# A decoder layer in three-pass float32: around three norms, low halves of weights are held back until the first low half of the operand is set down, and the next three are queued behind it

## The chip, the cores and the metric

One core of a Trainium2 chip. The metric is the device time of one execution of the whole program, in microseconds, from the program's start to its end; three executions were timed.

## The reference

One layer of a decoder, 256 tokens by 2048 channels, all in float32:

```
x  <- LN0(a*x + 0.5*(silu(x @ A1) * (x @ U1)) @ O1)       feed-forward, 5504 wide
z  =  x @ W_in                                            convolution, recurrence and gate parts
m  =  sigmoid(gc)*(yA @ Wa) + sigmoid(gh)*(yB @ Wb)       yA: gated convolution, yB: gated recurrence
x  <- LN1(a*x + m @ W_out)
x  <- LN2(a*x + 0.5*(silu(x @ A2) * (x @ U2)) @ O2)
x  <- LN3(a*x + sigmoid(x @ W_pg) * (p @ W_pp))
```

LN is a layer norm over the 2048 channels with a scale and a shift. All weights are read once from memory, 430 MB in all.

## The kernel before

**Three matmuls for one.** Every product is made of operands that are split in a high and a low half: the high half is the value rounded to the matmul's format (a cast on ScalarE), the low half is the rest (a subtraction on VectorE). A product is the sum of three matmuls into one bank: high by high, high by low, low by high. For the weights the high half is `wh` (`weight_cast`, L1141) and the low half `wl` (`weight_split`, L1153); a piece of both is 256 rows by 512 columns, and holds for 12 matmuls, six for each of the two row tiles of 128 tokens. For the operand, which is normalized and turned before, the halves are `xh` (L302) and `xl` (L303), both made in `halves`; one pair covers four blocks of 128 channels, 12 matmuls. Feed-forward operands are named `gh` and `gl`.

**Units.** `run_unit` goes through a unit, one block of 512 output columns: for each block of channels the row tile 0, then row tile 1, three matmuls for each block of 128 channels (`passes`, L1210 and L1214). When row tile 1 has used a piece of weights, its buffers come free, and `feed` loads, casts and splits the next pieces as far as there is room: 4 raw buffers, 6 and a few more for the halves. A raw buffer is free for the next load as soon as its split is done.

**A norm.** The last unit before a norm adds its result to `x0` (row tile 0) and `x1` (row tile 1), and takes statistics by blocks of 512 columns. `layer_norm` turns these to a mean and a factor `r`, normalizes four times 512 columns in place (L496), and puts off for each of the four quarters the making of an operand: four transposes on TensorE (L289), scale and shift on ScalarE out of the bank (L490, `y` or `yT`), the cast to `xh`, the subtraction to `xl`. The first quarter of row tile 0 is what the next unit's first matmuls need. Three norms have this form: the first behind the first feed-forward part, the second behind the mixer's output product, the third behind the second feed-forward part. At the third, small units (`ple_w_proj`, `pp`, L998) lie between the norm and the first unit that needs its operand. The closing norm has no operand and is another function.

**What sets the order.** The program is written in one stream, and a scheduler orders each engine's queue by a model of the times. `issue_after(i)` tells it to put an instruction behind `i`. The table `gate` holds such wishes: `gate["lo"]` has an instruction and a count, and each split that finds the count above zero is put behind that instruction (`gated`). In the kernel before, the first two splits behind a norm's second normalizing step of row tile 0 are held behind that step. On its engine each instruction then waits in order for what it needs. SP issues the loads, in order too.

Of the kernel before, what the change touches and what calls it, by code (L numbers as in the profile page):

```python
# [10 lines left out]
F32 = mybir.dt.float32  # L11
# [3 lines left out]
ALU = mybir.AluOpType  # L15
# [14 lines left out]
LATE = (4, 12)  # L30
# [8 lines left out]
class Stat:  # L39
# [3 lines left out]
    def __init__(self):  # L43
        self.parts = {}
# [7 lines left out]
class Unit:  # L52


    def __init__(self, stat, w, row, nk, col, width, epi, split=SPLIT):
        self.stat, self.w, self.row, self.nk = stat, w, row, nk
        self.col, self.width, self.epi = col, width, epi
        self.blocks = []
        k = 0
        for n in split:  # L60
            end = min(nk, k + n)
            if k < end:
                self.blocks.append([list(range(i, min(end, i + KG))) for i in range(k, end, KG)])
            k = end
# [78 lines left out]
def hybrid_layer(ctx: ExitStack, tc: tile.TileContext, x, p, ln_g, ln_b, ffn1_w_in, ffn1_w_out, mix_w_in,  # L143
                 conv_w, hg_lower_bound, hg_norm_w, branch_w_conv, branch_w_hgrn, mix_w_out,
                 ffn2_w_in, ffn2_w_out, ple_w_gate, ple_w_proj, x_t, p_t, small_t, out):
    nc = tc.nc

    def pool(name, bufs=1, **kw):
        return ctx.enter_context(tc.tile_pool(name=name, bufs=bufs, **kw))


    low = pool("low", side="left")
    wp = pool("wp", side="left")
    op = pool("op", side="left")
# [50 lines left out]
        used_at[n] = max(used_at.values()) + 1  # L205


    state = {"tick": 0}
    later = []
    unsettled = set()  # L210
    gate = {}
    background = deque()

    def defer(delay, fn):
        insort(later, (state["tick"] + delay, fn), key=lambda e: e[0])
# [70 lines left out]
    def transposed(src, nb):  # L286
        tp = ptile("t", "tp")
        for i in range(nb):
            state["turned"] = nc.tensor.transpose(tp[:, i * P : (i + 1) * P], src[:, i * P : (i + 1) * P], ident).ins  # L289
        return tp  # L290

    def halves(stat, t, g, src, nb, tag, into=None):

        if into:
            h, l = into
        else:
            where, bufs = {"s": (region["pool"], 7), "m": (region["pool"], 4)}.get(tag, (op, 8))
            h = where.tile([P, 4, P], F32R, tag=tag + "h", name=tag + "h", bufs=bufs)
            l = where.tile([P, 4, P], F32R, tag=tag + "l", name=tag + "l", bufs=bufs)
        hf = h[:, :nb, :].rearrange("p a b -> p (a b)")  # L300
        lf = l[:, :nb, :].rearrange("p a b -> p (a b)")
        state["half"] = nc.scalar.copy(hf, src).ins  # L302
        nc.vector.tensor_tensor(out=lf, in0=src, in1=hf.bitcast(F32), op=ALU.subtract)  # L303
        stat.parts[t, g] = (h, l)

    def to_stat(stat, t, g, src, nb, tag):
# [10 lines left out]
    def plain_tile(t, c):  # L317

        if c % 2 == 0:
            plain[t, c // 2] = high(("11", "12", "21", "22")[2 * t + c // 2], "yT")  # L320
        return plain[t, c // 2][:, c % 2, :]
# [128 lines left out]
    def moments(t, scale):  # L450

        mv = st.tile([P, 2], F32, tag="mv", name="mv", bufs=2)
        nc.vector.bn_aggr(mv, stats.pop(t))
        return mv[:, 0:1], rsqrt_of(mv[:, 1:2], 1, 1.0, LN_EPS / scale ** 2)
# [23 lines left out]
    def layer_norm(t, i, scale, stat):  # L478

        mean, r = moments(t, scale)  # L480

        def operand(c, xc):
            y = plain_tile(t, c) if stat is x2 else st.tile([P, CC], F32, tag="silu", name="y", bufs=2)
            tp = transposed(xc, 4)
            if t == 0 and c < 2:
                gate["pe"] = state["turned"], 1
            with tc.issue_after(state["half"]) if c else nullcontext():
                for a in range(4):
                    k = i * 16 + 4 * c + a
                    nc.scalar.activation(y[:, a * P : (a + 1) * P], tp[:, a * P : (a + 1) * P], AF.Identity,  # L490
                                         bias=gbT[:, 48 + k : 49 + k], scale=gbT[:, k : k + 1])
            halves(stat, t, c, y, 4, "x")

        for c in range(4):
            xc = xt[t][:, c * CC : (c + 1) * CC]
            norm = nc.vector.tensor_scalar(out=xc, in0=xc, scalar1=mean, scalar2=r, op0=ALU.subtract, op1=ALU.mult)  # L496
            defer((4 if t else 5) + c, lambda c=c, xc=xc: operand(c, xc))
            if c == 1 and t == 0:
                gate["lo"] = norm.ins, 2
        if t == NT - 1:  # L500
            for c in range(4):
                unsettled.add(c)
                early = stat is x2
                defer(2 + 3 * c if early else 40 + 20 * c, lambda c=c, early=early: affine_rows(i, c, early, stat))
# [496 lines left out]
    for c in range(4):  # L1001
        def epi_s(t, acc, c=c):
# [13 lines left out]
            if c == 3:  # L1016
# [3 lines left out]
                          split=LATE if c == 3 else LONG if c == 0 else SPLIT))  # L1020
# [36 lines left out]
    cur = {"cast": 0, "split": 0}  # L1057
# [26 lines left out]
    def may_load(ring):  # L1084
        if not loads[ring]:
            return False
        if ring == "raw":
            return taken["raw"] < NRAW
        key, kind = loads[ring][0][:2]
        if ring == "12" and not key[0].shorted:  # L1090
            return False
        return kind == region["kind"] and held["on"] and (held[ring] < HIGH[ring] or key in half)
# [30 lines left out]
    def addable():  # L1123
        if not adds:
            return False
        i = adds[0]
        el = plan[i]
        if i > cur["split"] + 1 or cur["split"] <= el["behind"] or any(key not in raws for key in el["add"]):
            return False
        return el.get("short") != "h2" or held["12"] < HIGH["12"]  # L1130
# [35 lines left out]
    def feed():  # L1166
        while True:
            ring = min((r for r in loads if may_load(r)), key=lambda r: first_use[loads[r][0][0]], default=None)
            if ring:
                weight_dma(ring)  # L1170
            elif addable():
                weight_add()
            elif castable():
                weight_cast()
            elif cur["split"] < cur["cast"]:
                weight_split()
            else:
                return
# [22 lines left out]
    def consumed(i):  # L1201
        pairs.pop(i)
        room[plan[i]["where"]] += 1
        feed()
# [11 lines left out]
    def run_unit(u, gi):  # L1216
        accs = {}
        for bi, blk in enumerate(u.blocks):
            for t in range(NT):
                if bi == 0:  # L1220
                    accs[t] = ptile("a", "acc")
                acc = accs[t][:, : u.width]
                for ii, ks in enumerate(blk):
                    tick()
                    for a, k in enumerate(ks):
                        passes(acc, u.stat, t, k, gi + ii, a, k == 0, k == u.nk - 1)
                    if t == NT - 1:
                        consumed(gi + ii)
                if bi == len(u.blocks) - 1:
                    u.epi(t, acc)  # L1230
            gi += len(blk)
        return gi
# [31 lines left out]
    gi = 0  # L1264
    for u in units:
        if isinstance(u, Unit):
            gi = run_unit(u, gi)
        elif isinstance(u, Quad):
            gi = run_quad(u, gi)
# [50 lines left out]
```

## Time and profile before

| | |
|---|---|
| median of 3 runs | 2201.24 us |
| lowest, highest | 2200.41, 2201.27 us |
| the profiled execution | 2200.81 us |
| its span, first to last instruction | 2199.1 us |
| busy: TensorE, its weight loads, VectorE, ScalarE | 99%, 82%, 83%, 54% |
| loads | 430 MB, 198 GB/s over the span |

The span is the time from the first to the last instruction; some 1.7 us lie around it. The busy time of TensorE is made of matmuls that overlap, so a wait is read better from the starts of two matmuls that follow each other than from the share.

### The profile page before, as it was taken

Reading aid. Unit: us, or ns where it says so; the run is one execution under the profiler, and the core shown is the slowest. Engines: PE = TensorE matmul, PEld = TensorE weight load, DVE = VectorE, ACT = ScalarE, POOL = GpSimd, SP = SyncE. Lnnn points to the kernel's source line nnn. Section 1 sums busy time; section 2 is a strip of 40 time slices with the busy share of each in tenths; the row PEclk is TensorE's granted clock in tenths of the full one; section 3 lists DMA queues with packets and bytes.
Section 4 is the critical chain, followed back from the end, with each engine's and each line's share of the span. In section 5 each row is a group of like instructions: output and inputs, shape, how many; then the busy total and the mean of one; then the engine's idle time right before and its main releaser. Section 6 shows DMA issues by size and latency. Waiting matters only on the chain.

```text
span 2199.1 us, 27091 instructions
## 1 busy us (share of the span) xinstructions
PE 2175.5 (99%) x9996; PEld 1811.4 (82%) x9996; DVE 1827.5 (83%) x2066; ACT 1182.8 (54%) x1412; POOL 20.0 (1%) x48
## 2 busy tenths in 40 slices
PE   9999999999999999999999999999999999999997
PEld 7988888888887888888888888798888888888886
DVE  6899999999886678657898888779999989998667
ACT  5555555555555534534565554645555555555463
POOL 1000000000000000000000000000000000000000
PEclk9999999999999999999999999999999999999999
DMA  8866666566663665554665676566666666665564
GB/s 263 265 193 200 210 204 194 186 201 211 208 194 116 197 216 178 185 181 153 220 203 177 202 244 210 171 210 201 192 200 189 203 211 201 201 210 176 192 221 144
DMA packets 228245, 436.29 MB, mean 198 GB/s; under 512 B 14608, under 2 KB 23312, under 8 KB 228112
## 3 DMA queue, kind: packets, MB, share of 16 engines
q1 hardware_dynamic: 226832, 430.37, 61.7%
q0 software_dynamic: 1280, 4.20, 0.5%
q8 instruction: 78, 1.28, 0.2%
q14 instruction: 55, 0.45, 0.1%
HBM read 430.31 MB, written 4.19 MB: 198 GB/s over the span
## 4 chain that ended last, share of the span: by engine, by line
PE 95%; DVE 2%; DMA 1%; ACT 1%; issue 1%; SPq 0%; DVEq 0%; ACTq 0%
PE bank L1214 61%; PE bank L1210 31%; PE bank L289 2%; PE bank L694 1%; DVE wl L1153 1%; DMA raw<-in_ffn_w_in_dram 1%; ACT wh L1141 1%; DMA raw<-in_ffn_w_out_dram 0%; DVE x L510 0%; DVE x L511 0%; PE bank L664 0%; ACT yT L490 0%; DVE x L496 0%; DVE raw L1119 0%; DVE bn L430 0%
## 5 line engine op out<-in xcount | busy, mean ns | idle before, releaser
L1141 ACT CAST wh<-raw 128x1024 fp32r<-128x1024 f32 (+2 forms) x975 | 975.9, 1030 | 763.0 <-PE bank L1214 331.3
L1153 DVE TENSOR_TENSOR wl<-raw,wh 128x1024 fp32r<-128x1024 f32 (+2 forms) x975 | 1140.9, 1197 | 237.1 <-ACT wh L1141 224.4
L1214 PE MATMUL bank<-wh,xl 128*128 128x512 f32 (+1 forms) x1624 | 625.6, 386 | 2.8 <-DVE xl L303 1.9
L1214 PE MATMUL bank<-wl,xh 128*128 128x512 f32 (+1 forms) x1624 | 625.9, 386 | 0.4 <-DVE wl L1153 0.4
L1210 PE MATMUL bank<-wh,xh 128*128 128x512 f32 (+1 forms) x1624 | 616.0, 387 | 0.4 <-ACT xh L302 0.4
L1214 PEld LDWEIGHTS bank<-wh,xl 128*128 128x128 f32 x1624 | 304.9, 188 | 63.3 <-DVE xl L303 4.0
L1210 PEld LDWEIGHTS bank<-wh,xh 128*128 128x128 f32 x1624 | 304.9, 188 | 58.9 <-ACT xh L302 1.5
L1214 PEld LDWEIGHTS bank<-wl,xh 128*128 128x128 f32 x1624 | 305.0, 188 | 58.6 <-DVE wl L1153 1.4
L1214 PE MATMUL bank<-wl,gh 128*128 128x512 f32 x896 | 348.5, 391 | 2.3 <-DVE wl L1153 2.3
L1214 PE MATMUL bank<-wh,gl 128*128 128x512 f32 x896 | 347.9, 390 | 0.0
L1210 PE MATMUL bank<-wh,gh 128*128 128x512 f32 x896 | 345.7, 392 | 0.0
L1119 DVE TENSOR_TENSOR raw<-raw,raw 128x1024 f32<-128x1024 f32 x216 | 254.7, 1180 | 12.4 <-DMA raw<-in_ffn_w_in_dram 6.7
L1214 PEld LDWEIGHTS bank<-wl,gh 128*128 128x128 f32 x896 | 168.3, 188 | 39.0 <-DVE wl L1153 4.8
L1210 PEld LDWEIGHTS bank<-wh,gh 128*128 128x128 f32 x896 | 168.1, 188 | 35.0 <-ACT wh L1141 0.4
L1214 PEld LDWEIGHTS bank<-wh,gl 128*128 128x128 f32 x896 | 168.2, 188 | 34.9
L1214 PE MATMUL bank<-wl,sh 128*128 128x512 f32 x464 | 181.6, 391 | 0.0
L1214 PE MATMUL bank<-wh,sl 128*128 128x512 f32 x464 | 180.5, 389 | 0.0
L1210 PE MATMUL bank<-wh,sh 128*128 128x512 f32 x464 | 177.1, 389 | 0.0
L1210 PEld LDWEIGHTS bank<-wh,sh 128*128 128x128 f32 x464 | 87.1, 188 | 18.3
L1214 PEld LDWEIGHTS bank<-wh,sl 128*128 128x128 f32 x464 | 87.1, 188 | 17.8
L1214 PEld LDWEIGHTS bank<-wl,sh 128*128 128x128 f32 x464 | 87.1, 188 | 17.8
L302 ACT CAST gh<-bank 128x512 fp32r<-128x512 f32 (+1 forms) x52 | 30.1, 578 | 75.9 <-PE bank L289 75.4
(184 smaller groups left out, 1121.5 us busy)
## 6 DMA issues: line engine op xcount, KB each, us to landing
raw<-in_ffn_w_in_dram SPq DMA_DIRECT2D x287, 512.0 KB, 4.4
raw<-in_mix_w_in_dram SPq DMA_DIRECT2D x176, 512.0 KB, 4.6
raw<-in_ffn_w_out_dram SPq DMA_DIRECT2D x168, 512.0 KB, 4.8
raw<-in_ffn_w_in_dram SPq DMA_DIRECT2D x66, 256.0 KB, 2.9
raw<-in_mix_w_out_dram SPq DMA_DIRECT2D x32, 512.0 KB, 4.7
raw<-in_ple_w_gate_dram SPq DMA_DIRECT2D x32, 512.0 KB, 4.9
raw<-in_ffn_w_in_dram SPq DMA_DIRECT2D x32, 384.0 KB, 4.0
raw<-in_branch_w_conv_dram SPq DMA_DIRECT2D x16, 512.0 KB, 5.1
```

The source lines that it names most:

```text
L289: state["turned"] = nc.tensor.transpose(tp[:, i * P : (i + 1) * P], src[:, i * P : (i + 1) * P], ident).ins
L302: state["half"] = nc.scalar.copy(hf, src).ins
L694: nc.tensor.matmul(gp[:, (h * 2 + t) * 64 : (h * 2 + t + 1) * 64], kd[:, h, t * P : (t + 1) * P], qd[:, h, t, :], start=True, stop=True)
L1119: nc.vector.tensor_tensor(out=out, in0=a, in1=b, op=ALU.add)
L1141: nc.scalar.copy(h[:, ks, :w], raw[:, ks, :w])
L1153: state["split"] = nc.vector.tensor_tensor(out=l[:, ks, :w], in0=raw[:, ks, :w], in1=h[:, ks, :w].bitcast(F32), op=ALU.subtract).ins
L1210: nc.tensor.matmul(acc, sh, wh[:, a, :n], start=first, stop=False)
L1214: nc.tensor.matmul(acc, x_part, w_part[:, a, :n], start=False, stop=last and i == 1)
```

## The change

Four edits. `run_unit` marks the last units before a norm (`last`, by their split of the channels, `LATE` or `(12,)`); when row tile 0 of such a unit begins its last block, it sets a number of splits that may still be written: to the end of this unit and two pieces on. `feed` writes no split once that number is used up, and so frees no raw buffer for further loads there. `lead` takes the place of `operand` as what is put off: it makes the operand, and for the first quarter of row tile 0 it then lifts the limit, sets `gate["lo"]` to the low half just written with a count of three, and calls `feed`. `halves` keeps its subtraction in `state["low"]` for that.

```diff
 class Unit: __init__
+        self.last = split in (LATE, (12,))
...
-    state = {"tick": 0}
+    MANY = 1 << 30
+    state = {"tick": 0, "splits": MANY}
...
 def halves
-        nc.vector.tensor_tensor(out=lf, in0=src, in1=hf.bitcast(F32), op=ALU.subtract)
+        state["low"] = nc.vector.tensor_tensor(out=lf, in0=src, in1=hf.bitcast(F32), op=ALU.subtract).ins
...
 def layer_norm
+        def lead(c, xc):
+            operand(c, xc)
+            if t == 0 and c == 0:
+                state["splits"] = MANY
+                gate["lo"] = state["low"], 3
+                feed()
...
-            defer((4 if t else 5) + c, lambda c=c, xc=xc: operand(c, xc))
+            defer((4 if t else 5) + c, lambda c=c, xc=xc: lead(c, xc))
...
 def feed
-            elif cur["split"] < cur["cast"]:
+            elif cur["split"] < cur["cast"] and state["splits"] > 0:
+                state["splits"] -= 1
                 weight_split()
...
 def run_unit
+                if u.last and t == 0 and bi == len(u.blocks) - 1:
+                    state["splits"] = gi + len(blk) + 2 - cur["split"]
```

Instructions are neither added nor taken away. The order differs only around the three norms, and between them it is the same. The lines of the changed kernel stand 3 (`halves`) to 11 (`passes`) further down.

VectorE at the first norm, from behind the normalizing of row tile 0 to the second low half; `wl` is a split of weights, `xl` a low half of the operand, `x1` the addition to row tile 1. Before:

```order
L1153 TENSOR_TENSOR wl_5645<-raw_5518,wh_5644 128x1024
L1153 TENSOR_TENSOR wl_5663<-raw_5530,wh_5662 128x1024
L1153 TENSOR_TENSOR wl_5675<-raw_5548,wh_5674 128x1024
L808 MEMSET uT_6836 128x4x2
L303 TENSOR_TENSOR xl_5690<-y_5680,xh_5689 128x512
L600 TENSOR_TENSOR x1_97<-x1_97,bank6_87 128x512
L430 BN_STATS bn_5370<-x1_97 128x6
L453 BN_AGGR mv_5726<-bn_5370 128x2
L1153 TENSOR_TENSOR wl_5719<-raw_5574,wh_5718 128x1024
L438 TENSOR_SCALAR w_5728<-mv_5726 128x1
L440 TENSOR_SCALAR m_5729<-mv_5726 128x1
L303 TENSOR_TENSOR xl_5709<-y_5699,xh_5708 128x512
```

And now:

```order
L818 MEMSET uT_6836 128x4x2
L306 TENSOR_TENSOR xl_5678<-y_5668,xh_5677 128x512
L1163 TENSOR_TENSOR wl_5645<-raw_5518,wh_5644 128x1024
L1163 TENSOR_TENSOR wl_5660<-raw_5530,wh_5659 128x1024
L1163 TENSOR_TENSOR wl_5685<-raw_5548,wh_5684 128x1024
L610 TENSOR_TENSOR x1_97<-x1_97,bank6_87 128x512
L1163 TENSOR_TENSOR wl_5719<-raw_5574,wh_5718 128x1024
L306 TENSOR_TENSOR xl_5709<-y_5699,xh_5708 128x512
L433 BN_STATS bn_5370<-x1_97 128x6
L306 TENSOR_TENSOR xl_5765<-y_5755,xh_5764 128x512
```

The first `xl` has moved ahead of three splits; the statistics, the aggregate and two small steps of row tile 1 have moved behind the second `xl`. TensorE's order is the same here.

VectorE at the second norm, the same piece. Before:

```order
L1153 TENSOR_TENSOR wl_11130<-raw_11013,wh_11129 128x1024
L1153 TENSOR_TENSOR wl_11213<-raw_11025,wh_11212 128x1024
L1153 TENSOR_TENSOR wl_11216<-raw_11055,wh_11215 128x1024
L1153 TENSOR_TENSOR wl_11222<-raw_11067,wh_11221 128x1024
L303 TENSOR_TENSOR xl_11163<-yT_11153,xh_11162 128x512
L980 SCALAR_TENSOR_TENSOR x1_10356<-x1_10356,bank3_84 128x512
L1153 TENSOR_TENSOR wl_11228<-raw_11133,wh_11227 128x1024
L303 TENSOR_TENSOR xl_11181<-yT_11153,xh_11180 128x512
L430 BN_STATS bn_10851<-x1_10356 128x6
L1153 TENSOR_TENSOR wl_11234<-raw_11219,wh_11233 128x1024
```

And now:

```order
L1163 TENSOR_TENSOR wl_11130<-raw_11013,wh_11129 128x1024
L306 TENSOR_TENSOR xl_11163<-yT_11153,xh_11162 128x512
L1163 TENSOR_TENSOR wl_11213<-raw_11025,wh_11212 128x1024
L1163 TENSOR_TENSOR wl_11216<-raw_11055,wh_11215 128x1024
L1163 TENSOR_TENSOR wl_11222<-raw_11067,wh_11221 128x1024
L990 SCALAR_TENSOR_TENSOR x1_10356<-x1_10356,bank3_84 128x512
L1163 TENSOR_TENSOR wl_11228<-raw_11133,wh_11227 128x1024
L306 TENSOR_TENSOR xl_11181<-yT_11153,xh_11180 128x512
L433 BN_STATS bn_10851<-x1_10356 128x6
L306 TENSOR_TENSOR xl_11270<-yT_11260,xh_11269 128x512
```

The first `xl` has moved ahead of three of four splits, and the third `xl` ahead of a split that stood between it and the statistics. On ScalarE the casts for two later pieces (`wh_11233`, `wh_11239`) moved behind the third operand's cast.

TensorE at the third norm, where the first group of six matmuls of the projection units ends (`gh_16424` is row tile 0, `gh_16440` row tile 1). Before:

```order
L1214 MATMUL bank0_81<-wl_16685,gh_16424 128x512
L1214 MATMUL bank0_81<-wh_16684,gl_16425 128x512
L1210 MATMUL bank4_85<-wh_16684,gh_16440 128x512
L1214 MATMUL bank4_85<-wl_16685,gh_16440 128x512
L1214 MATMUL bank4_85<-wh_16684,gl_16441 128x512
```

And now:

```order
L1225 MATMUL bank0_81<-wl_16685,gh_16424 128x512
L1225 MATMUL bank0_81<-wh_16684,gl_16425 128x512
L1221 MATMUL bank7_88<-wh_16696,gh_16424 128x512
L1225 MATMUL bank7_88<-wl_16697,gh_16424 128x512
L1225 MATMUL bank7_88<-wh_16696,gl_16425 128x512
```

The group of row tile 1 into `bank4` has moved two groups back, and the last group of row tile 1 (`wh_16770`) has moved behind the gate unit's first 24 matmuls; the group into `bank7`, whose former content ScalarE copies out (`pp_16885`), comes second. On ScalarE one cast of weights (`wh_16906`) moved from ahead of the first operand's cast to behind the third. On VectorE the first `xl` is now the first instruction behind the normalizing, with three splits behind it. On SP four loads of norm rows (`gb`, from `ln_g`) now stand ahead of the next load of weights, where they stood behind three of them. The transposes of row tile 1 stand two together and then one, where each stood alone.

## Rows read from the trace of the kernel before

**Rows 1.** Busy time of the engines over the whole span, from the page: us, share of the span, instructions.

```profile
PE 2175.5 (99%) x9996; PEld 1811.4 (82%) x9996; DVE 1827.5 (83%) x2066; ACT 1182.8 (54%) x1412; POOL 20.0 (1%) x48
```

**Rows 2.** The chain that ended last, from the page: share of the span by engine.

```profile
PE 95%; DVE 2%; DMA 1%; ACT 1%; issue 1%; SPq 0%; DVEq 0%; ACTq 0%
```

**Rows 3.** Busy time by engine in the stretches around the three norms that the change touches. Columns: stretch, its length, busy us of each engine with its instructions, granted clock, DMA share, GB/s.

```profile
690.00:712.00 22.00, 20.27 (x102) 15.58 (x100) 16.43 (x32) 17.53 (x40) 0.95 (x1) 1.00 0.29 96
1386.00:1412.00 26.00, 22.59 (x109) 17.43 (x109) 20.91 (x35) 21.38 (x42) 0.00 (x0) 1.00 0.56 182
2076.00:2116.00 40.00, 40.00 (x192) 32.98 (x192) 26.13 (x44) 32.58 (x63) 0.00 (x0) 1.00 0.53 178
```

**Rows 4.** TensorE in order of time at the first norm: start, us, line, operation, output and inputs, count; in brackets its idle time before and who ended it.

```profile
695.53 0.40 PE L1214 MATMUL bank<-wl,xh 128*128 128x512 f32 x1
696.10 0.51 PE L1214 MATMUL bank<-wh,xl 128*128 128x512 f32 x1 [0.17 <-DVE xl L303]
...
698.74 0.39 PE L1214 MATMUL bank<-wl,xh 128*128 128x512 f32 x1
699.52 0.50 PE L1214 MATMUL bank<-wh,xl 128*128 128x512 f32 x1 [0.39 <-DVE xl L303]
...
704.64 1.04 PE L289 MATMUL bank<-ident,x 128*128 128x128 f32 x8
706.84 0.66 PE L289 MATMUL bank<-ident,x 128*128 128x128 f32 x4 [1.16 <-ACT y L490]
707.49 0.50 PE L1210 MATMUL bank<-wh,xh 128*128 128x512 f32 x1
```

**Rows 5.** TensorE in order of time at the second norm.

```profile
1392.21 0.40 PE L1214 MATMUL bank<-wl,xh 128*128 128x512 f32 x1
1393.89 0.50 PE L1214 MATMUL bank<-wh,xl 128*128 128x512 f32 x1 [1.29 <-DVE xl L303]
...
1396.75 0.40 PE L1214 MATMUL bank<-wh,xl 128*128 128x512 f32 x1
...
1399.36 0.40 PE L1214 MATMUL bank<-wl,xh 128*128 128x512 f32 x1
1400.66 0.51 PE L1214 MATMUL bank<-wh,xl 128*128 128x512 f32 x1 [0.90 <-DVE w L438]
...
1407.30 1.04 PE L289 MATMUL bank<-ident,x 128*128 128x128 f32 x8
```

**Rows 6.** VectorE in order of time at the first norm.

```profile
690.11 1.92 DVE L496 TENSOR_SCALAR x<-x,mv,r 128x512 f32<-128x512 f32 x4
691.94 3.49 DVE L1153 TENSOR_TENSOR wl<-raw,wh 128x1024 fp32r<-128x1024 f32 x3
695.37 0.68 DVE L303 TENSOR_TENSOR xl<-y,xh 128x512 fp32r<-128x512 f32 x1
...
695.97 0.68 DVE L600 TENSOR_TENSOR x<-x,bank 128x512 f32<-128x512 f32 x1
696.68 0.69 DVE L430 BATCH_NORM_STATS2 bn<-x 128x6 f32<-128x512 f32 x1
...
697.59 1.16 DVE L1153 TENSOR_TENSOR wl<-raw,wh 128x1024 fp32r<-128x1024 f32 x1
...
698.78 0.68 DVE L303 TENSOR_TENSOR xl<-y,xh 128x512 fp32r<-128x512 f32 x1
```

**Rows 7.** ScalarE: the cast that the first low half waits for, at the first and at the second norm.

```profile
693.48 0.62 ACT L302 CAST xh<-y 128x512 fp32r<-128x512 f32 x1
...
1390.37 0.62 ACT L302 CAST xh<-yT 128x512 fp32r<-128x512 f32 x1
```

**Rows 8.** VectorE in order of time at the second norm.

```profile
1388.61 4.62 DVE L1153 TENSOR_TENSOR wl<-raw,wh 128x1024 fp32r<-128x1024 f32 x4
1393.16 0.68 DVE L303 TENSOR_TENSOR xl<-yT,xh 128x512 fp32r<-128x512 f32 x1
...
1395.81 0.69 DVE L303 TENSOR_TENSOR xl<-yT,xh 128x512 fp32r<-128x512 f32 x1
```

**Rows 9.** The third norm: VectorE's first split behind the normalizing, three pieces of ScalarE, and the matmuls that open the second and the third group of six of the projection units on TensorE.

```profile
2080.00 1.22 DVE L1153 TENSOR_TENSOR wl<-raw,wh 128x1024 fp32r<-128x1024 f32 x1
...
2085.90 1.06 ACT L1141 CAST wh<-raw 128x1024 fp32r<-128x1024 f32 x1
2086.84 0.64 ACT L302 CAST xh<-y 128x512 fp32r<-128x512 f32 x1
...
2089.68 1.11 ACT L998 COPY pp<-bank 128x512 f32<-128x512 f32 x2
...
2089.24 0.40 PE L1210 MATMUL bank<-wh,gh 128*128 128x512 f32 x1
...
2090.63 0.39 PE L1210 MATMUL bank<-wh,gh 128*128 128x512 f32 x1
```

**Rows 10.** Stretches behind the last matmul, columns as in rows 3.

```profile
2185.00:2190.00 5.00, 0.31 (x2) 0.00 (x0) 4.86 (x11) 2.08 (x3) 0.00 (x0) 1.00 0.57 210
2190.00:2195.00 5.00, 0.00 (x0) 0.00 (x0) 4.89 (x10) 0.00 (x0) 0.00 (x0) 0.53 0.23 85
```

**Rows 11.** Loads: the whole span, from the page, and a stretch of the third norm, columns as in rows 3.

```profile
DMA packets 228245, 436.29 MB, mean 198 GB/s; under 512 B 14608, under 2 KB 23312, under 8 KB 228112
...
2090.00:2095.00 5.00, 5.00 (x23) 4.00 (x22) 2.95 (x7) 5.00 (x12) 0.00 (x0) 1.00 0.98 340
```

## The prediction

> **What bounds the kernel now.** I read the engines' busy time first. TensorE is busy in 99% of the span, VectorE in 83% [rows 1], and 95% of the chain that ended last is TensorE [rows 2]. So a change among VectorE's instructions moves the end only where TensorE stands idle. Next come the stretches around the three norms that the change touches. TensorE's busy time falls short of the stretch by 1.73 us at the first norm (690 to 712), by 3.41 us at the second (1386 to 1412), and by nothing at the third (2076 to 2116) [rows 3]. Then the single instructions of the first two stretches, to see who is waited for. In TensorE's rows the time from one matmul's start to the next is what to look at: about 0.23 us when nothing waits, and 0.34 for the first step behind a wait.
>
> At the first norm TensorE waits twice for a low half of the operand (xl): 696.10 comes 0.57 behind 695.53, and 699.52 comes 0.78 behind 698.74. A third wait, for the activations of the other row tile (706.84), is of another kind: transposes, an activation, a cast, 2.85 us from 704.64 to 707.49 [rows 4]. At the second norm the two waits for xl are longer: 1.68 us up to 1393.89 and 1.30 up to 1400.66 [rows 5]. Each beyond 0.23, and 0.11 more for the slow step behind it, the four waits are worth 0.45 + 0.66 + 1.56 + 1.18 = 3.85 us. That is all that can be won here, 0.17% of the time; what a measurement of this kernel can tell from no change is about 0.2%, 4.4 us.
>
> **First norm.** VectorE finishes the four normalizing steps at 692.03, then does three splits of weights (3.49 us), and only then the first xl, at 695.37 [rows 6]. The cast that this xl needs ends at 693.48 + 0.62 = 694.10 [rows 7]. Now VectorE sits idle from 692.03 to 694.13, does xl to 694.81, and TensorE, which wants it at 695.76, doesn't wait: 0.45 us won. The three splits start at 694.73 and cost 1.14 us each (back to back), so they end at 698.15. The weights that they make are wanted from 698.26 on, since two tiles of the next unit were split already: no new wait for wl.
>
> But the second xl stands behind them. The order puts the x1 addition (0.60 to the next start) and one more split (1.14) ahead of it, while the statistics (696.68), the aggregate and two small steps, which were ahead of it, go behind it. So xl starts at 698.15 + 0.60 + 1.14 = 699.89 and ends at 700.57. Before, it started at 698.78 and TensorE took it at 699.52 [rows 4, 6]. TensorE takes it at 700.60 now: 1.08 us late, net, with the 0.45 spent. Put otherwise: VectorE's new idle time is 2.10 us, the work taken out from ahead of the second xl is about 1.0 us. The other row tile's normalizing now ends near 705.6 with its first two quarters at 704.3 and 704.7, while TensorE turns them at 704.64 + 1.08 = 705.72, so nothing is added there. The 2.85 us chain follows unchanged. **+1.08 us.**
>
> **Second norm.** One split stays ahead of the first xl here and three go behind. The four splits ran from 1388.61 on, xl at 1393.16 [rows 8]. Now the first split ends near 1389.83, and xl waits for the cast that ends at 1390.37 + 0.62 = 1390.99 [rows 7]: it runs 1391.02 to 1391.71, ahead of TensorE's wish at 1392.44. The wait of 1.56 us goes. Behind it three splits (1391.62, 1392.76, 1393.90), the x1 addition at 1395.04, another split at 1395.64, and the second xl at 1396.79, to 1397.47; before it ran at 1395.81 [rows 8]. TensorE's fifth row block, which took that xl at 1396.75 without a wait, gets it at 1397.50 now. Meanwhile the third xl is no longer behind two splits and ends near 1398.7, well ahead of its use at about 1400.3, so the wait of 1.18 us goes. From 1396.75 to the transposes at 1407.30 it took 10.55 us [rows 5]; now 10.55 - 1.18 + 0.11 = 9.48 from 1397.50, which is 1406.98. **-0.32 us.** A new wait takes back most of what the two old ones give.
>
> **Third norm.** No wait stood there: the matmuls of the small projection units fill the time. Three things move. ACT's cast of 1.06 us at 2085.90 falls out from ahead of the operand's cast (2086.84), so what follows on ACT comes 0.8 us earlier: the first copy out of a projection's bank, which started at 2089.68, starts at 2088.89 and ends at about 2089.5. TensorE's order now has the matmuls that need this very bank second instead of third: they are due at 2089.24, not 2090.63 [rows 9]. That costs a wait of about 0.25 and the slow step, 0.35 us. Second, the other row tile's transposes stood apart among matmuls; now two quarters stand together, with six matmuls (1.4 us) ahead of the third. The chain of 2.85 us seen at the first norm [rows 4] is then covered by 12 transposes (1.1) and those 1.4 only, so some 0.4 of it shows, 0.5 with the slow steps. Bounds: nothing, if these transposes come with projection matmuls still to do, and 1.5, if nothing covers but the transposes. I take 0.5. Third, the raw weights' buffers come free 7 us later, because the split that frees the first one starts at about 2087.3 in place of 2080.0 [rows 9]. On SP's queue that load now stands behind four loads of norm rows. I cost it at nothing (covered by the weights already in place) and give the other case below. **+0.85 us.**
>
> **Sum.** +1.08 - 0.32 + 0.85 = +1.6 us. The profiled execution took 2200.81 us (2199.1 of span and 1.7 around it), so 2202.4; the median of the runs, 2201.24, is 0.4 above it, so 2202.8 us. TensorE has no gap behind these places that would take it back, and its last matmul sets the closing norm.
>
> **The clock.** The wait at the first norm grows to some 2.3 us from start to start, longer than any of before in the middle of the kernel. The granted clock is 1.00 (the level of 2.4 GHz) over all three stretches [rows 3], and after the last matmul, with TensorE idle from 2185.3, it is still 1.00 up to 2190 and 0.53, most of it the level of 1.2 GHz, in the slice behind [rows 10]. So the row speaks for no loss. The Trainium skill, "TensorE: Matmul & The Clock Gate", section "HAM oscillation — how this bites in real kernels", says that waits between bursts of matmuls can throttle the array, and that each such burst then starts at half speed. By it a wait of ours could cost more than its length; the trace shows such a fall behind the last matmul alone.
>
> **The rivals.**
> - *The low half alone was the wait.* If the scheduler's order costs less than I think, the first xl's waits (0.45 + 1.56) go and the second xl's stay as they were: 2201.24 - 2.0 = 2199.2; with all four gone 2197.4. For it: xl is what ended those waits. Against: VectorE works in order, and the second xl is behind the held splits at both places. Chance 0.1.
> - *Slower: late weights at the third norm.* From 2086 on, eight loads of 256 KB and four of 512 KB (4.2 MB) stand together. The engines of the queue moved 340 GB/s at 98% there before [rows 11], so they need 12.3 us and end near 2099 to 2101, ahead of the last tile's first use, 66 matmuls and 8 transposes behind 2089.24 and so near 2105.5, by a cast and a split (2.3 us) and some 2 us more. Were they to get the mean of 198 GB/s [rows 11], 21 us would pass, and the last weights land near 2107.5, ready at 2110: TensorE would wait 4.5 us, 2207.3 in all. It decides from a landing at about 2103 on. Chance 0.08.
> - *Slower: the clock falls behind the new wait.* Then the 36 matmuls of the first unit's row tile (8.2 us) would take twice as long: 2211. Chance 0.02.
> - *The third norm stays covered:* 2202.0, within my case's own range.
>
> **How the numbers follow.** My case has 0.8 and its own range is 2201.0 to 2204.8: -0.3 at the second norm may be 0, the third norm is 0 to 1.9, and the runs differ by 0.9. The first rival's lower half is outside of the range, as is most of the late weights' case: 2199.6 to 2205.4. All of my case lies within 0.2% of 2201.24 (2196.8 to 2205.6); of the first rival almost all; of the slower two, three quarters lie beyond. That makes faster 0.02, same 0.9, slower 0.08.
>
> **What would show it.** Right: at the first norm a single wait for xl, from about 698.5 to 700.6, in place of two, and VectorE idle for 2 us behind the normalizing; at the second norm no wait for the first and third xl, one of 1.5 to 2 us for the second near 1397.5; at the third a short wait for a projection's copy and one at the other row tile's first operand. Wrong: TensorE's idle time smaller than before at the first norm, a matmul that waits for wl or for a load, or a clock under 1.00 between 690 and 2185.

## The result and the profile after

| | kernel before | changed kernel |
|---|---|---|
| median of 20 runs each | 2200.70 us | 2204.68 us |
| lowest, highest | 2199.48, 2202.39 | 2200.89, 2207.65 |
| ratio of the runs, 95% interval | | 1.0017 (1.0010 to 1.0024) |
| the profiled execution's span | 2199.1 us | 2202.9 us |

The median is 1.9 us above the forecast of 2202.8 and inside its range (2199.6 to 2205.4); the change is within 0.2%, as forecast. But the forecast had +1.6 us, and +4.0 came. The runs also lie further apart, 6.8 us in place of 2.9.

The page of the changed kernel, to be held against [rows 1, 2]:

```profile
PE 2178.3 (99%) x9996; PEld 1813.5 (82%) x9996; DVE 1826.4 (83%) x2066; ACT 1183.0 (54%) x1412; POOL 20.3 (1%) x48
...
PE 92%; DVE 4%; ACT 1%; issue 1%; DMA 1%; SPq 0%; DVEq 0%; ACTq 0%
```

TensorE is busy 2.8 us longer with the same 9996 matmuls. A wait can't do that; matmuls that take longer can. The stretches of [rows 3] say where. Columns: stretch, length, busy us and instructions by engine, granted clock, DMA share, GB/s.

```profile
690.00:712.00 22.00, 18.90 (x87) 14.57 (x86) 14.25 (x28) 14.76 (x35) 0.95 (x1) 0.92 0.29 96
1386.00:1412.00 26.00, 23.93 (x108) 18.82 (x106) 19.61 (x36) 20.60 (x36) 0.00 (x0) 0.93 0.58 181
2076.00:2116.00 40.00, 39.86 (x190) 32.26 (x188) 22.38 (x39) 27.72 (x55) 0.00 (x0) 1.00 0.48 165
```

The granted clock, 1.00 in all three before, is 0.92 and 0.93 in the first two. VectorE at the first norm did what the working said (compare [rows 6]): its second xl was due at 699.89 and came at 699.55, in an execution that was 0.33 us earlier up to there.

```profile
693.81 0.69 DVE L306 TENSOR_TENSOR xl<-y,xh 128x512 fp32r<-128x512 f32 x1 [2.08 <-ACT xh L305]
694.41 3.49 DVE L1163 TENSOR_TENSOR wl<-raw,wh 128x1024 fp32r<-128x1024 f32 x3
697.82 0.68 DVE L610 TENSOR_TENSOR x<-x,bank 128x512 f32<-128x512 f32 x1
698.42 1.22 DVE L1163 TENSOR_TENSOR wl<-raw,wh 128x1024 fp32r<-128x1024 f32 x1
699.55 0.68 DVE L306 TENSOR_TENSOR xl<-y,xh 128x512 fp32r<-128x512 f32 x1
```

The first xl is early, and the second stands behind three splits, the x1 addition and a fourth split. TensorE there (compare [rows 4]): start, length, line, operation, count, and in brackets the idle time and its ender.

```profile
697.96 0.39 PE L1225 MATMUL bank<-wl,xh 128*128 128x512 f32 x1
700.29 0.50 PE L1225 MATMUL bank<-wh,xl 128*128 128x512 f32 x1 [1.94 <-DVE xl L306]
...
701.09 0.51 PE L1225 MATMUL bank<-wh,xl 128*128 128x512 f32 x1
701.40 0.63 PE L1221 MATMUL bank<-wh,xh 128*128 128x512 f32 x1
701.83 0.63 PE L1225 MATMUL bank<-wl,xh 128*128 128x512 f32 x1
...
704.74 0.40 PE L1225 MATMUL bank<-wh,xl 128*128 128x512 f32 x1
...
707.05 1.04 PE L292 MATMUL bank<-ident,x 128*128 128x128 f32 x8
709.25 0.66 PE L292 MATMUL bank<-ident,x 128*128 128x128 f32 x4 [1.16 <-ACT y L493]
```

One wait for xl in place of two, as forecast. Then comes what the sum did not have: three matmuls run at their usual pace, and from 701.09 the steps are 0.31 and then 0.43. From 701.09 to 704.74 nine steps take 3.65 us, where nine of 0.23 take 2.07: 1.6 us lost while TensorE was never idle. The same time in fine stretches, columns as above:

```profile
698.00:700.00 2.00, 0.35 (x2) 0.00 (x0) 2.00 (x3) 0.65 (x2) 0.00 (x0) 1.00 0.95 351
700.00:702.00 2.00, 1.71 (x6) 1.38 (x7) 1.82 (x6) 1.67 (x6) 0.00 (x0) 0.81 0.94 325
702.00:704.00 2.00, 2.00 (x7) 1.52 (x6) 1.78 (x6) 0.54 (x2) 0.00 (x0) 0.50 0.72 251
704.00:706.00 2.00, 2.00 (x9) 1.64 (x8) 1.29 (x3) 0.00 (x0) 0.00 (x0) 0.84 0.03 5
706.00:708.00 2.00, 2.00 (x14) 1.59 (x12) 0.00 (x0) 0.31 (x1) 0.00 (x0) 1.00 0.00 0
```

The clock is at its lower level (0.50, 1.2 GHz) behind the wait, not in it, and back at 1.00 while the same stream of matmuls goes on. The second norm has the same picture (compare [rows 5]):

```profile
1397.88 0.40 PE L1225 MATMUL bank<-wl,xh 128*128 128x512 f32 x1
1399.92 0.50 PE L1225 MATMUL bank<-wh,xl 128*128 128x512 f32 x1 [1.65 <-DVE xl L306]
...
1400.95 0.61 PE L1221 MATMUL bank<-wh,xh 128*128 128x512 f32 x1
1401.36 0.63 PE L1225 MATMUL bank<-wl,xh 128*128 128x512 f32 x1
...
1404.35 0.41 PE L1225 MATMUL bank<-wh,xl 128*128 128x512 f32 x1
...
1410.77 1.04 PE L292 MATMUL bank<-ident,x 128*128 128x128 f32 x8
```

From 1400.95 to 1404.35 eight steps take 3.40 us in place of 1.84. The waits for the first and the third xl are gone as forecast, and TensorE takes the second at 1399.92. The forecast was 1397.50, and this norm began 2.42 us later than in the kernel before. At the third norm the two small stalls came that were forecast, and no wait for a weight:

```profile
2092.08 0.40 PE L1225 MATMUL bank<-wh,gl 128*128 128x512 f32 x1
2092.61 0.50 PE L1221 MATMUL bank<-wh,gh 128*128 128x512 f32 x1
...
2109.96 0.60 PE L292 MATMUL bank<-ident,x 128*128 128x128 f32 x4
2110.56 0.50 PE L1221 MATMUL bank<-wh,xh 128*128 128x512 f32 x1
```

The step to 2092.61, the first matmul into the bank that ScalarE has to copy out, is 0.53 us where 0.23 is usual. The step to 2110.56, the first use of the other row tile's operand, is 0.60 where 0.35 is usual behind four transposes.

**Three stretches as a measure.** One execution can't be set against another as a whole: TensorE reached the first norm between 689.8 and 692.3 us in the executions below, although no instruction differs up to there. So each norm is measured by TensorE's own starts: N1 from the first group of transposes of row tile 0 to the first of row tile 1 (before 690.75 to 704.64, after 690.42 to 707.05), N2 likewise (1387.42 to 1407.30, 1389.84 to 1410.77), N3 from the first transposes to the last matmul (2083.32 to 2184.93, 2086.39 to 2188.77). "Fall" means steps of 0.43 us behind the wait. Two runs of the later series that took several thousand us are left out of all counts and medians.

| execution | N1 | N2 | N3 | fall at |
|---|---|---|---|---|
| before | 13.89 | 19.88 | 101.61 | |
| changed | 16.63 | 20.93 | 102.38 | N1, N2 |
| after_again, the changed kernel | 15.01 | 19.33 | 102.38 | none |
| after_paired, the changed kernel | 16.63 | 19.32 | 102.36 | N1 |
| first_only | 16.61 | 19.71 | 101.60 | N1 |
| second_only | 13.90 | 19.31 | 101.81 | none |
| third_only | 13.90 | 19.76 | 102.37 | none |
| fill_wait | 15.00 | 19.46 | 102.38 | none |
| fill_paired | 15.00 | 19.45 | 102.39 | none |
| two_first | 13.50 | 20.13 | 101.58 | none |
| high_first | 12.77 | 19.86 | 101.58 | none |
| high_first_after | 13.64 | 19.26 | 102.39 | none |
| best_of_both | 12.77 | 19.27 | 101.61 | none |

Where the order around a norm is that of the kernel before, N1 is 13.89 or 13.90, N3 101.58 to 101.81, and N2 19.71 to 20.13: a difference at the second norm is good to some 0.2 us.

### The profile page after: what moved, and what is told of

Same layout as the page of the kernel before. It is cut to its first block, busy times and chain, and to the rows that moved or that the text cites. A ratio compares the mean times of both kernels' runs of the same rounds, so it can differ in the third digit from the quotient of the medians.

```text
span 2202.9 us, 27085 instructions
## 1 busy us (share of the span) xinstructions
PE 2178.3 (99%) x9996; PEld 1813.5 (82%) x9996; DVE 1826.4 (83%) x2066; ACT 1183.0 (54%) x1412; POOL 20.3 (1%) x48
## 4 chain that ended last, share of the span: by engine, by line
PE 92%; DVE 4%; ACT 1%; issue 1%; DMA 1%; SPq 0%; DVEq 0%; ACTq 0%
PE bank L1225 60%; PE bank L1221 30%; DVE wl L1163 2%; PE bank L292 2%; PE bank L704 1%; ACT wh L1151 1%; DVE raw L1129 1%; DMA raw<-in_ffn_w_in_dram 1%; DMA raw<-in_ffn_w_out_dram 0%; ACT y L493 0%; DVE x L520 0%; DVE x L521 0%; PE bank L674 0%; ACT yT L493 0%; ACT xh L305 0%
```

## The experiments

**Each norm alone.** Three kernels, each with the limit on splits and the new hold at one norm only; nothing else moves.

```diff
+    HELD = (0,)
...
-            if t == 0 and c == 0:
+            if t == 0 and c == 0 and i in HELD:
...
-                    state["splits"] = gi + len(blk) + 2 - cur["split"]
+                    state["norm"] += 1
+                    if state["norm"] in HELD:
+                        state["splits"] = gi + len(blk) + 2 - cur["split"]
```

> The change at the first norm alone. Theory 1, the queue alone: the second low half comes about 1.1 us later net, and the time is 2200.7 + 1.1 = 2201.8, with a granted clock of 1.00 over 690 to 712. Theory 2, the queue and the clock: TensorE's new wait of about 2 us drops the granted clock, some eight or nine matmuls behind it take 0.43 us in place of 0.23, 1.6 us more: 2203.4, with a granted clock near 0.92 over 690 to 712 and 1.00 in all other stretches between the warm-up and the end. Theory 3, the added time lies at the third norm (late weights, the projection's copy): 2200.7, no change here.

Measured: 2203.17 us median of 11, the kernel before on the same chip 2200.97; ratio 1.0010 (1.0001 to 1.0018), +2.2 us. Its profiled execution has the fall at the first norm and none at the second, columns as above:

```profile
690.00:712.00 22.00, 18.91 (x88) 14.89 (x88) 13.81 (x29) 14.62 (x33) 0.95 (x1) 0.92 0.29 96
1386.00:1412.00 26.00, 23.86 (x114) 18.92 (x113) 21.02 (x37) 19.76 (x34) 0.00 (x0) 1.00 0.56 182
```

N1 is 2.72 longer, N3 as before. The first norm by itself brings the fall, so theory 3 (all of it at the third norm) is out. The median lies between theory 1 and theory 2; the profiled execution, at 2205.08, is the slowest of the 11.

> The change at the second norm alone. Theory 1, the queue alone: two waits for a low half go, one of 1.65 us comes, net -0.5 us: 2200.2, granted clock 1.00 over 1386 to 1412. Theory 2, the queue and the clock: the same order, and 1.6 us more for eight matmuls at the lower level: 2201.8, granted clock near 0.93 in that stretch and 1.00 at the first norm. Theory 3, the added time lies at the third norm: as theory 1.

Measured: 2201.39, ratio 1.0001 (0.9992 to 1.0010), between theory 1 and theory 2; the profiled execution, at 2199.31, is one of its fastest. The profile showed something that no theory had. TensorE behind the wait:

```profile
1394.80 0.40 PE L1226 MATMUL bank<-wl,xh 128*128 128x512 f32 x1
1396.84 0.50 PE L1226 MATMUL bank<-wh,xl 128*128 128x512 f32 x1 [1.64 <-DVE xl L307]
...
1406.07 1.04 PE L293 MATMUL bank<-ident,x 128*128 128x128 f32 x8
```

The wait is that of the changed kernel to 0.01 us (1.64 idle beside 1.65, 2.04 from start to start in both), and all steps behind it are 0.23. The same wait in the same stream of work brought the fall in one execution and not in another. From 1396.84 to 1406.07 it took 9.23 us; in the changed kernel, from 1399.92 to 1410.77, 10.85. That is the price of one fall: 1.6 us.

> The change at the third norm alone. Theories 1 and 2 agree: a wait of 0.3 us for a projection's copy out of its bank and the slow step behind it, 0.4 together, and 0.4 to 0.5 where two quarters of the other row tile's operand stand together: 2200.7 + 0.8 = 2201.5, the granted clock 1.00 throughout. Theory 3, the added time lies here: 2203 or more, with a wait for a weight that was loaded late.

Measured: 2201.51, ratio 1.0002 (0.9994 to 1.0011); N3 is 0.76 longer and no matmul there waits for a weight. By that stretch the order at the third norm costs what was expected of it; the median, 0.5 above the kernel before, is not clear of the noise.

**The changed kernel once more.**

> The changed kernel as it is, a second look. Queue and clock: the two waits are 1.9 and 1.65 again; behind each the granted clock either falls (1.6 us more in the stretch: 16.6 at the first norm, 20.9 at the second) or does not (15.0 and 19.3), since the runs scatter by 7 us; the time is 2202.2 and 1.6 more for each fall. If the fall comes behind every wait of this length: 16.6 and 20.9 again, 2204.5 to 2205.

Measured: 2203.55 us, a single run. TensorE at the first norm:

```profile
699.44 0.39 PE L1225 MATMUL bank<-wl,xh 128*128 128x512 f32 x1
701.76 0.50 PE L1225 MATMUL bank<-wh,xl 128*128 128x512 f32 x1 [1.93 <-DVE xl L306]
...
706.90 1.04 PE L292 MATMUL bank<-ident,x 128*128 128x128 f32 x8
```

The wait is 1.93 us, 0.01 less than in the first execution, and the 22 matmuls from its end on ran at 0.23: N1 is 15.01, N2 19.33, no fall at either place. So the unchanged program shows both outcomes, and without falls its three stretches are 1.12 longer, 0.55 shorter and 0.77 longer than before. The mean clock that each run lists (to three places) agrees. In the profiled executions of the table it is 0.998 without a fall, 0.997 with one and 0.996 with two. 0.996 is listed for 9 of the 32 runs of the changed kernel. It is listed for none of the 98 runs of the other kernels here and for none of the 86 runs of the kernel before beside them. In the first series the eight runs at 0.996 have a median of 2205.28, the nine at 0.997 of 2204.07, and the three at 0.998 of 2201.61.

**The waits filled.** Eight more matmuls in TensorE's order ahead of the first one that needs the second xl, at the first and the second norm; their result is not read.

```diff
+    filled = []
+    FILL = 8
...
+            if i == 1 and t == 0 and k == 4 and w and stat in (x1, x2) and stat not in filled:
+                filled.append(stat)
+                spare = banks[min(role_of["a"], key=lambda b: used_at[b])]
+                for _ in range(FILL):
+                    nc.tensor.matmul(spare[:, :n], sh, wh[:, a, :n], start=True, stop=True)
```

> The changed kernel, with eight more matmuls (0.23 us each, into a free bank that nobody reads) in TensorE's order ahead of the first matmul that needs the second low half, at the first and at the second norm. VectorE's and ScalarE's orders stay. Theory 1, the queue alone: the wait is filled and ends when it ended, nothing is won: 2204.7, or up to 0.5 us above where the eight are longer than the wait. Theory 2, the queue and the clock: the waits end when they ended but the granted clock stays at 1.00 behind them, and 2 x 1.6 us fall away: 2201.5, with no step over 0.35 us between the matmuls behind the two waits, and runs that scatter as little as those of the kernel before (3 us in place of 7). Theory 3: as theory 1.

> The changed kernel again, timed on the same chip as the two runs beside it. The order of the three norms is worth +1.1 - 0.6 + 0.8 = +1.3 us by the stretches of the earlier runs. Queue and clock: a median 3 to 4 us above the kernel before, and in the profile each of the two waits with or without the fall (16.6 or 15.0 us at the first norm, 20.9 or 19.3 at the second). The queue alone: +1.3.

> The changed kernel with the two waits filled by eight idle matmuls each, on the same chip. Queue and clock: 1.3 to 1.5 us above the kernel before, 1.5 to 2.5 below the changed kernel beside it, and stretches of 15.0 and 19.5 us with a granted clock of 1.00. If the clock is not the cause: equal to the changed kernel beside it within 0.5 us.

Measured, fill_wait: 2203.07 beside 2200.97 (ratio 1.0011, 1.0002 to 1.0020). In the pair, on another chip, 2203.69 for the filled kernel and 2203.19 for the changed one beside it, with the same ratio to the kernel before for both, 1.0011 (1.0002 to 1.0020). In the trace it is as the clock theory says, TensorE at the first norm in fill_wait:

```profile
698.13 0.39 PE L1232 MATMUL bank<-wl,xh 128*128 128x512 f32 x1
698.36 1.98 PE L1231 MATMUL bank<-wh,xh 128*128 128x512 f32 x8
700.46 0.50 PE L1232 MATMUL bank<-wh,xl 128*128 128x512 f32 x1
...
705.60 1.04 PE L294 MATMUL bank<-ident,x 128*128 128x128 f32 x8
```

The wait is filled, N1 is 15.00 in both profiled executions, and no fall is seen. But the times miss the expectation. The filled kernel should have been 1.5 to 2.5 us below the changed one, and it is level with it; the changed kernel should have been 3 to 4 us above the kernel before, and it is 2.2 above. Two things stand against the test. On that chip the changed kernel seems to have had fewer falls than in its first series: one run of 11 lists 0.996 and five 0.998, and the profiled execution had one fall. And the filled kernel lies 2.1 and 2.7 us above the kernel before, where its stretches add up to 1.11 - 0.42 + 0.77 = 1.5; the rest was not explained. (A part of it lies between N1 and N2 in the two profiled executions: 683.34 and 683.00 us there, 682.78 to 682.83 in all the others.)

What a fall costs is thus shown in the traces, execution by execution; the medians of the two kernels side by side don't show it. The runs of one kernel, parted by the clock that they list, point the same way as the traces. The changed kernel's five runs at 0.998 on that chip have a median of 2202.1, its six others 2205.1; first_only's seven at 0.998 have 2202.5, its four others 2204.6. In the filled kernel the same two parts lie 0.3 and 0.1 us apart, in the kernel before beside them -0.2 to 1.1. That is not proof for a single run, since 0.997 is listed for runs of kernels without such a wait too. By this reading the changed kernel without a fall is 1.1 us above the kernel before, near the 1.3 of its stretches, and what stays unexplained is why the filled kernel is slower than that.

**The second low half ahead of the third split,** at the first norm alone; the edit is against first_only.

```diff
-            if t == 0 and c == 0 and i in HELD:
-                state["splits"] = MANY
-                gate["lo"] = state["low"], 3
+            if t == 0 and c < 2 and i in HELD:
+                state["splits"] = MANY if c else 2
+                gate["lo"] = state["low"], 2
                 feed()
```

> The change at the first norm alone, but with the second low half ahead of the third held split (two splits behind the first low half, then the addition, the second low half, and the other splits). The queue theory: the first low half is early as in the changed kernel, the second is set down near 697.9, before TensorE wants it at 698.2, so both waits of before (0.45 and 0.66) go and none comes: 2201.0 - 1.1 = 2199.9, the stretch from the first to the second group of transposes 12.8 us in place of 13.89, the granted clock 1.00. Rival: the third or fourth split then comes too late for its matmul, TensorE waits for wl, and the time is 2201 or more.

Measured: 2200.84 beside 2201.30, ratio 0.9997 (0.9988 to 1.0006). VectorE, and then TensorE:

```profile
697.27 0.69 DVE L307 TENSOR_TENSOR xl<-y,xh 128x512 fp32r<-128x512 f32 x1
697.87 2.36 DVE L1164 TENSOR_TENSOR wl<-raw,wh 128x1024 fp32r<-128x1024 f32 x2
700.14 0.69 DVE L434 BATCH_NORM_STATS2 bn<-x 128x6 f32<-128x512 f32 x1
700.74 1.28 DVE L307 TENSOR_TENSOR xl<-y,xh 128x512 fp32r<-128x512 f32 x2
```

```profile
700.68 0.39 PE L1226 MATMUL bank<-wl,xh 128*128 128x512 f32 x1
701.48 0.51 PE L1226 MATMUL bank<-wh,xl 128*128 128x512 f32 x1 [0.41 <-DVE xl L307]
...
703.91 1.17 PE L293 MATMUL bank<-ident,x 128*128 128x128 f32 x8
```

The second xl came at 697.27, in time for TensorE (698.18). But two splits and the statistics now stand ahead of the third xl, and TensorE waits for that: N1 is 0.39 shorter, not 1.1. The rival (a late wl) is wrong too; the wait moved one low half on. Of the 1.1 us that the two old waits cost, 0.7 was handed to the next piece in the queue.

**TensorE's order in place of VectorE's.** For the first row tile behind the first and second norm, the eight matmuls of a quarter that use xh go ahead of the four that use xl.

```diff
...
+                        four = []
+                        for jj in (ii, ii + 1):
+                            tick()
+                            for a, k in enumerate(blk[jj]):
+                                high_pair(acc, u.stat, t, k, gi + jj, a, k == 0)
+                                four.append((k, gi + jj, a))
+                        for k, w, a in four:
+                            low_pair(acc, u.stat, t, k, w, a, k == u.nk - 1)
```

> The kernel before, with its VectorE and ScalarE orders kept, but at the first and second norm the first row tile takes its products in another order: for each quarter the eight matmuls with the high half (xh), then the four with the low half (xl), so that xl is wanted 1.38 us later. If what TensorE lacks there is the low half alone, the waits of 0.45 and 0.66 at the first norm go and those of 1.56 and 1.18 at the second shrink to 0.2 and 0: 2201.0 - 3.6 = 2197.4. Rival: the weights' low halves, which the eight matmuls now take 0.46 us earlier, become the wait, and little is won: 2200 to 2201.

> The changed kernel with the same order of products as in the run beside it. Queue and clock: the waits for the second low half shrink from 2.1 and 1.8 to 0.7 and 0.4, the granted clock stays at 1.00, and the sum at the three norms is -0.3, -1.9 and +0.8 against the kernel before: 2199.5. The queue alone (the waits cost 4 us by themselves): 2204.7 - 2.8 = 2201.9. In either case it stays behind high_first by some 2 us, since the held splits still stand ahead of the second low half.

Measured: 2200.36 for the first (ratio 0.9995, 0.9986 to 1.0004) and 2201.50 for the second (1.0000, 0.9991 to 1.0008), beside 2201.30; expected were 2197.4 and 2199.5. At the first norm both came out as expected (N1 1.12 and 0.25 shorter). At the second neither did: 0.02 and 0.62 shorter in place of 2.5 and 1.9. The first one there, ScalarE and then TensorE:

```profile
1395.48 2.00 ACT L1142 CAST wh<-raw 128x1024 fp32r<-128x1024 f32 x2
1397.36 0.63 ACT L303 CAST xh<-yT 128x512 fp32r<-128x512 f32 x1
```

```profile
1398.05 0.50 PE L1211 MATMUL bank<-wh,xh 128*128 128x512 f32 x1 [0.75 <-ACT xh L303]
1401.34 1.01 PE L1223 MATMUL bank<-wh,xh 128*128 128x512 f32 x2 [0.27 <-ACT wh L1142]
```

With the waits for xl covered, TensorE waits for the high half, which stands behind two casts of weights on ScalarE, and then for such a cast itself. My reading that only the low half was missing holds at the first norm and not at the second. high_first_after has no fall; its longest step at the second norm is 1.26 us. It lies 0.2 us above the kernel before, though it holds the whole change: its stretches sum to -0.25 - 0.62 + 0.78 = -0.1.

**The parts that pay.** The change at the second norm alone, with the new order of matmuls at both; the first line is against first_only, and the order is the edit above.

```diff
-    HELD = (0,)
+    HELD = (1,)
```

> The change at the second norm alone, and at the first and second norm the first row tile's products with the high half ahead of those with the low half, by quarters. By the stretches of the earlier runs -1.1 at the first norm, -0.6 at the second, nothing at the third, no wait over 0.8 us and so no fall of the clock: 1.7 us below the kernel before, and the lowest of all. Rival: the waits for ScalarE's casts that took the place of those for the low half at the second norm take the 0.6 back: 1.1 below.

Measured: 2199.05 beside 2200.99, ratio 0.9989 (0.9980 to 0.9998), and the lowest of all: N1 1.12 and N2 0.61 shorter, N3 as before, 1.7 in all against 1.9 measured. That is 0.09%, below what one comparison of this kernel can surely tell, but it is the sum of two stretches that each came out as worked out. The order of matmuls adds nothing at the second norm: N2 is 19.27, and 19.31 in second_only without it.

## Why the prediction was right in kind and short in size

- **First norm, +1.08.** Measured without a fall +1.12 (after_again), +1.11 (both filled kernels). Each step held: xl without a wait at first, the second one behind three splits, an addition and a fourth split, the chain of the other row tile unchanged (1.16 us of idle time in both).
- **Second norm, -0.32.** Measured -0.55 and -0.57. The forecast moment of the second xl was met (2.04 from start to start). The old wait up to 1400.66 was read rightly as one for xl, though its row names w L438: that xl ran from 1399.92 to 1400.60. The 0.25 more is mostly two small stalls of before, 0.09 at 1399.04 and 0.12 at 1403.52, which went as well; it is hardly more than N2 varies by.
- **Third norm, +0.85.** Measured +0.77: 0.41 for the bank that waits for its copy (0.35 forecast), and 0.5 at the other row tile's operand as forecast, less about 0.1 because two groups of transposes stand together and have one slow step less behind them.
- **Late weights at the third norm (a rival).** Didn't come: no matmul at the third norm waited for a weight. The loads did not stand together as the working had it; SP issued them one after another from 2090.0 to 2108.9, in an execution 3.07 us later at this place. From 2090 to 2110 the mean is 266 GB/s (184, 272, 393 and 214 in stretches of 5 us), between my bounds of 198 and 340; only the fastest stretch is above both, columns as in the stretches above:

```profile
2100.00:2105.00 5.00, 5.00 (x24) 4.14 (x23) 2.92 (x5) 3.19 (x5) 0.00 (x0) 1.00 1.05 393
```

  Two casts of weights on ScalarE waited for a load, 0.55 us at 2100.32 and 0.56 us at 2103.02; no matmul did.

- **The clock: the step that failed.** The prediction read the row behind the last matmul (TensorE idle, 1.00 up to 2190, the lower level after that) and said "So the row speaks for no loss". It gave the fall a chance of 0.02 and a price of 8.2 us, 36 matmuls at double length. Both were wrong. Among the profiled executions with a wait unshortened, the fall came behind that of the first norm in three of four (changed, after_paired, first_only; not after_again) and behind that of the second in one of four (changed; not after_again, after_paired, second_only). Its price is 1.6 us, because the clock returns while the stream goes on: eight or nine matmuls are slow, not 36. What misled me is that the row of an engine that goes idle and stays idle shows when its clock is taken down there; it says nothing about an engine that takes up work again, and here the level changed 0.93 to 1.18 us after it had, in the four falls. The rule of the Trainium skill, "TensorE: Matmul & The Clock Gate", section "HAM oscillation — how this bites in real kernels", that waits between bursts can make the next burst start slow, was cited and overruled. The trace agrees with it in kind only: the waits in the page's example are longer than these, and the burst starts at full speed here and turns slow after three or four matmuls.
- **The sum.** 1.12 - 0.56 + 0.77 = 1.3 us without falls, where 1.6 was forecast. The profiled execution has two falls, 3.2 more; the rest of its 3.8 us (-0.7) lies outside of the three stretches. The median of +4.0 in the first series is 2.7 above 1.3. That would be 1.7 falls a run (2.7 by 1.6), if nothing else is in it; on another chip the median was +2.2. That 2204.68 lies inside the range is luck in part: the room above 2202.8 was there for the third norm, the scatter of the runs and late weights, and what filled it was the clock. How often the fall comes, and why the filled kernel is not faster than the changed one, stays open.

## What to carry to other kernels

When an operation is put first in a queue that has no gaps, look for who gets its old place: here the second low half paid for the first, and when that was mended, the third. A wait of about 2 us in an otherwise unbroken stream of matmuls costs more than its length at times; put its price down with a second term, and see whether several short waits become one long one, even where their sum shrinks. Where TensorE itself has work that doesn't need the late piece, moving that work into the wait can do more than moving the other engine's queue: 1.12 us at the first norm here, though nothing at the second, where another piece was late too.

## What was not expected of the hardware

The same program, with the same waits to 0.01 us, shows the lower clock behind a wait in one execution and not in the next: at the second norm 10.85 us from the wait's end to the transposes, or 9.24 (after_again, 1399.77 to 1409.01). The longest of the second norm's waits, 2.06 us from start to start in after_paired, had no fall behind it. What decides between the two was not found. In all of the executions, no such fall stands behind the shorter waits at these places, as the 1.68 us from start to start of the kernel before [rows 5] or the 0.75 us of idle time above.
